# Attention steps in rounds of two, split first maxima, and roots as plain products, in a hybrid diffusion block

## The chip, the cores and the metric

The kernel runs on one core of one Trainium2 chip. The time is device microseconds of one execution of the whole program; lower is better. Before the change it is 1875.17 us, the median of three runs (1874.18 to 1875.43).

The engines have short names in the profile: PE is TensorE (PEld its weight loads), DVE VectorE, ACT ScalarE, POOL GpSimd, SP the engine that issues transfers. PE multiplies a stationary operand (weights, up to 128 rows and 128 columns) with a moving one and writes into banks of its result memory, of 512 fp32 columns each. A product with fewer rows or columns uses a part of the array, and the profile names the form: `128*128` is the whole array, `64*128` one half of the rows, `128*64` one half of the columns.

## What is computed

Two layers over 512 latent and 256 context tokens of width 1024: grouped-query attention with normed and rotated queries and keys, then a bidirectional Mamba-2 mixer, each followed by a gated feed-forward layer. The change touches attention, and the row norms of all layers.

```python
def rms_norm(x, g):
    xf = x.astype(jnp.float32)
    y = xf * lax.rsqrt(jnp.mean(xf * xf, axis=-1, keepdims=True) + EPS)
    return (y * g.astype(jnp.float32)).astype(x.dtype)

def gqa_attend(q, k, v):
    s = jnp.einsum('bqhgd,bkhd->bhgqk', q, k).astype(jnp.float32) * (HEAD_DIM ** -0.5)
    p = jax.nn.softmax(s, axis=-1).astype(v.dtype)
    return jnp.einsum('bhgqk,bkhd->bqhgd', p, v)

    q_l = rms_norm(q_l.reshape(bsz, seq, N_HEADS, HEAD_DIM), q_norm)
...
    k_all = jnp.concatenate([k_l, k_c], axis=1)
    v_all = jnp.concatenate([v_l, v_c], axis=1)
...
    ob = lax.map(lambda qblk: gqa_attend(qblk, k_all, v_all), qb)
```

There are 16 query heads of 64 channels and 4 key heads. Latent queries see all 768 keys, context queries the 256 context keys.

## The kernel before

Tokens lie along columns, channels along partitions. fp32 operands of the large products are split into a high and a low part of a faster type (float32r), and each product is three: high by high, low by high, high by low (`mm3`, lines 108, 109, 111). Products that stay in plain fp32 show as two PE records each; transposes and float32r products as one.

**Heads in pairs.** Two query heads lie on the two halves of the partitions, so that their score products use the two halves of the array's rows. A `Pair` has two generators:

- `maxima` finds, for each query, a bound of its scores ahead of the exponentials. It has seven parts; each writes score products (`ps_m`, line 625) into a two-bank buffer, and DVE reduces it to maxima (line 627). At the end the row `diag` is made of them (line 648).
- `steps` has seven steps, one for each block of 128 keys for latent queries, and a last one for context queries. A step makes the scores transposed (`ps_s`, lines 697 and 699: eight products of 512 columns, the last two add the maxima from `diag`), ACT takes the exponential into `pr` (line 700), and DVE adds it to `acc`. The step hands back a function, `later`, that multiplies `pr` with the values (`ps_o`, `ps_oc`, line 661) and, at the end, divides by the sums (`ps_sum`).

**The loop** (line 809) goes over eight pairs. For each step t of pair p it emits the step's scores, then one part of the next pair's maxima, then the `later` of the step before, so that the exponential has a step's time. Then comes other work: the preparation of queries of later pairs (`prep`), and fill: projections of queries (`ps_q`), modulation products (`ps_ada`), and in pairs 6 and 7 the output projection (`ps_d`).

**Buffers.** The result memory has two two-bank buffers (`S`), taken in turn by `ps_s` and `ps_m`, and four single banks (`Bank`), for `ps_o`, `ps_q`, `ps_ada`, sums and roots.

**Roots.** `rstd_rows` (line 235) gives the reciprocal roots of mean squares. Per token they come out as columns; they are needed as rows, equal over 128 partitions (c = 1, the norms of whole tokens: tiles rsa, `rsTa`, `rsTf`, `rsTs`, `rsTy`) or over each half of 64 (c = 2, head norms: `rsTq`, ten times six). A transpose of a column that is repeated 128 times does it (line 266). For c = 2 DVE first writes the repeated columns out into a wide tile, `rbq` (line 259).

**What sets the order.** Within an engine, instructions run in the order of the program. Where the kernel gives no order by hand, a scheduler sets it from the order of emission and from its own estimates; `behind(a, b)` keeps a behind b.

Of the kernel before, what the change touches and what calls it, by code (L numbers as in the profile page):

```python
# [7 lines left out]
P = 128  # L8
# [3 lines left out]
ALU = mybir.AluOpType  # L12
AX = mybir.AxisListType
# [54 lines left out]
def t3(g, name, dt=F32, n=T):  # L68
    return g.t3p.tile([P, n], dt, tag="t3", bufs=g.n3, name=name)
# [165 lines left out]
def rstd_rows(g, sq, n, cols, width, name, bank):  # L235

    nc = g.nc
    c = cols.shape[-1]  # L240
    nt = n // P
    ps = bank(f"ss{name}")
    for t in range(nt):
        nc.tensor.matmul(ps[:, t * c : (t + 1) * c], sq[:, t * P : (t + 1) * P], cols, start=True, stop=True)
    small = lambda nm: g.p.tile([P, nt * c], F32, tag="rst", bufs=8, name=nm)
    a, y, u = small("rsa"), small("rsy"), small("rsu")
    nc.vector.tensor_scalar(a, ps[:, : nt * c], 1.0 / width, EPS, ALU.mult, ALU.add)

    for f in ((lambda: nc.scalar.activation(y, a, AF.Ln)), (lambda: nc.scalar.activation(y, y, AF.Exp, scale=-0.5))):
        follow(g, f()) if g.tables else f()  # L250
    nc.vector.tensor_tensor(u, y, a, ALU.mult)
    nc.vector.scalar_tensor_tensor(u, y, -0.5, u, ALU.mult, ALU.mult)
    if c == 1:
        nc.vector.scalar_tensor_tensor(a, u, 1.5, y, ALU.add, ALU.mult)
        root = lambda t: a[:, t : t + 1].broadcast_to([P, P])
    else:
        rb = t3(g, f"rb{name}", n=n)
        wide = lambda v: v.unsqueeze(2).broadcast_to([P, nt * c, P // c])
        nc.vector.scalar_tensor_tensor(rb.rearrange("p (a b) -> p a b", b=P // c), wide(u), 1.5, wide(y),
                                       ALU.add, ALU.mult)  # L260
        root = lambda t: rb[:, t * P : (t + 1) * P]
    yield BREAK
    for t0 in range(0, nt, 4):
        pt = bank(f"rsT{name}")
        for t in range(t0, min(nt, t0 + 4)):
            nc.tensor.transpose(pt[:, (t - t0) * P : (t - t0 + 1) * P], root(t), g.ident)
        yield (pt, t0 * P, min(n, (t0 + 4) * P))


# [122 lines left out]
def attention(g, fill, X, late):  # L392


    nc, I = g.nc, g.I
# [209 lines left out]
        nc.gpsimd.tensor_copy(id2[h], g.ident[h, h])  # L605
    small = lambda name, dt=F32: g.p.tile([P, 2, T // P], dt, tag="mx", bufs=4, name=name)

    class Pair:


# [4 lines left out]
        def maxima(self):  # L615


            qh, kh = qprep[self.p][0], [h for h, _ in k2[self.kv]]
            lat, ctx, mz = small("ma"), small("mb"), small("mz")

            def scores(ts, k0, n, out):
                ps = Sb("ps_m")
                for i, t in enumerate(ts):
                    for e in range(2):
                        nc.tensor.matmul(ps[:, 512 * e + n * i : 512 * e + n * i + n], qh[S64[e], t * P : (t + 1) * P],
                                         kh[e][S64[e], k0 : k0 + n], start=True, stop=True)
                nc.vector.reduce_max(out[:, :, ts[0] : ts[-1] + 1], ps.rearrange("p (e t k) -> p e t k", e=2, k=n),
                                     axis=AX.X, negate=True)

            scores((4, 5), L, C, lat)  # L630
            nc.vector.tensor_copy(ctx[:, :, 4:], lat[:, :, 4:])
            yield
            for t in (0, 2):
                scores((t,), 0, L, lat)
                yield
                scores((t + 1,), 0, L, lat)
                yield
                scores((t, t + 1), L, C, ctx)
                if t:

                    for e in range(2):
                        for h in range(2):
                            nc.vector.tensor_tensor(mz.rearrange("p h t -> p t h")[S64[e], :, h], lat[S64[h], e],
                                                    ctx[S64[h], e], ALU.min)
                    self.diag = g.t3p.tile([P, T], F32R, tag="mrow", bufs=2, name=f"diag{self.p}")
                    v = self.diag.rearrange("p (t h q) -> p t h q", h=2, q=64)
                    for h in range(2):
                        nc.vector.tensor_tensor(v[:, :, h], id2.unsqueeze(1).broadcast_to([P, T // P, 64]),
                                                mz[:, h].unsqueeze(2).broadcast_to([P, T // P, 64]), ALU.mult)
                yield  # L650

        def steps(self):
# [5 lines left out]
            def values(po, pr, t, off, n, first, last):  # L658
                v = vt[t][:, self.kv * HD : (self.kv + 1) * HD]
                for e in range(2):  # L660
                    nc.tensor.matmul(po[S64[e], :n], v, pr[:, 512 * e + off : 512 * e + off + n], start=first, stop=last)  # L661

            def final(po, ps, acc, out):

# [25 lines left out]
            for t in range(7):  # L690
                ps, pr = Sb("ps_s"), g.t3p.tile([P, 1024], F32, tag="pr", bufs=3, name="pr")
                for q0, n, k0, off in (((0, L, t * P, 0),) if t < 6 else ((L, C, L, 0), (L, C, L + P, C))):
                    q, k = slice(q0, q0 + n), slice(k0, k0 + P)
                    outs = [ps[:, 512 * e + off : 512 * e + off + n] for e in range(2)]
                    for i, (a, b) in enumerate(((0, qh), (1, qh), (0, ql))):
                        for e in range(2):
                            nc.tensor.matmul(outs[e], kk[e][a][S64[e], k], b[S64[e], q], start=i == 0, stop=False)  # L697
                    for e in range(2):
                        nc.tensor.matmul(outs[e], onesr[S64[e]], self.diag[S64[e], q], start=False, stop=True)  # L699
                exps.append(nc.scalar.activation(pr, ps, AF.Exp))  # L700
# [12 lines left out]
                yield (lambda t=t, pr=pr, po=po, acc=acc: later_lat(po, pr, t, acc)) if t < 6 else (  # L713
                    lambda pr=pr, acc=acc: later_ctx(pr, acc))
# [25 lines left out]
    def ofetch(p):  # L740
        od[p] = t3(g, f"od{p}")
        nc.sync.dma_start(od[p], odram[p])
# [66 lines left out]
    for p in range(NH // 2):  # L809
        m = iter(())  # L810
        if p < 7:
            m = pairs[p + 1].maxima()
        for t, todo in enumerate(pairs[p].steps()):
            next(m, None)
            if late_step:
                late_step()
            late_step = todo
            if p < 6:
                if t in (0, 3, 4, 5):
                    next(prep[p])  # L820
                if t == 6:
                    for _ in prep[p]:
                        pass
                    if p == 5:
                        ofetch(0)
                spread(1.04 if p < 5 else 0.62)
                continue
            if p == 6 and t < 5:
                if t < 4:
                    ofetch(t + 1)  # L830
                osplit(t)
                wos.append(load_w(g, I["w_o"][t * P : (t + 1) * P], after=exps[-1]))
            if p == 6 and t == 2:
                late(wos[:3], (0, 1, 2))
            if p == 6 and t == 4:
                late(wos[3:], (3, 4))
            if p == 7 and t == 2:
                ofetch(5)
            if p == 7 and t == 3:
                osplit(5)  # L840
                osplit(6)
            if p == 6 and t < 3:
                spread(0.62)
                if t == 2:
                    for _ in side:
                        pass
                    for _, gen in tails:
                        for _ in gen:
                            pass
            else:  # L850
                fill.run(3.5)
    late_step()
    osplit(7)

# [675 lines left out]
```

## Time and profile before

| | |
|---|---|
| median of three runs | 1875.17 us |
| the profiled execution | 1875.38 us |
| its span, first to last instruction | 1873.6 us |
| granted TensorE clock | 0.998 |
| attention with heads (the loop over pairs) | about 111 to 367 us of the span |

A row of the timeline has start and duration in us, engine, line, operation, output and inputs, the form of the array, the shape, and how many equal ones are merged in it. Matmuls are pipelined, so durations overlap: what a product holds PE for is the difference of two starts. A row of a group has, behind the bar, busy us and mean ns of one, then the idle time in front of it and what ended it.

### The profile page before, as it was taken

How to read it: one execution, taken by the hardware profiler on the slowest of the kernel's cores; microseconds unless marked ns; L12 is line 12 of the kernel's file. 1: busy time of each engine (PE TensorE's matmuls, PEld its weight loads, DVE VectorE, ACT ScalarE, POOL GpSimd, SP SyncE). 2: the span in 40 equal slices, each digit the busy share in tenths (PEclk: the TensorE clock that was granted, in tenths of full speed). 3: DMA queues.
4: the chain of work that ended last, by engine and by line, in shares of the span. 5: the costliest groups of instructions: out<-in, count | busy, mean ns of one | idle time of the engine just before them, and what ended most of it. 6: DMA issues, size and time to landing. Idle time of an engine off the chain costs nothing.

```text
span 1873.6 us, 28798 instructions
## 1 busy us (share of the span) xinstructions
PE 1848.9 (99%) x11474; PEld 1547.2 (83%) x11474; DVE 1303.6 (70%) x1950; ACT 807.3 (43%) x1402; POOL 299.8 (16%) x266
## 2 busy tenths in 40 slices
PE   9999999999999999999999999999999999999999
PEld 8876656798888888888888888888887888888887
DVE  6588888778787776544487787777797565565655
ACT  4534444363122222222367667776666352323231
POOL 2123120040000000000032333444443210000000
PEclk9999999999999999999999999999999999999999
DMA  9233151124444552211224432443352223222232
GB/s 345 76 109 101 63 178 52 57 84 164 146 135 145 191 185 99 68 58 56 68 91 141 124 105 87 124 124 113 124 178 93 79 91 97 95 95 97 90 103 89
DMA packets 74070, 211.67 MB, mean 113 GB/s; under 512 B 9040, under 2 KB 14544, under 8 KB 73808
## 3 DMA queue, kind: packets, MB, share of 16 engines
q1 hardware_dynamic: 73936, 209.84, 34.0%
q8 instruction: 90, 1.47, 0.3%
q14 instruction: 44, 0.36, 0.1%
HBM read 198.79 MB, written 6.82 MB: 110 GB/s over the span
## 4 chain that ended last, share of the span: by engine, by line
PE 84%; DVE 7%; issue 3%; DMA 2%; POOL 2%; ACT 2%; SPq 0%; DVEq 0%; POOLq 0%; ACTq 0%
PE ps_up L108 10%; PE ps_up L111 10%; PE ps_up L109 10%; PE ps_d L108 6%; PE ps_d L111 6%; PE ps_d L109 6%; PE ps_in L111 4%; PE ps_in L109 4%; PE ps_in L108 4%; PE ps_s L697 2%; PE ps_o L661 2%; PE ps_st L1123 2%; DMA wada<-in_adaA 1%; PE ps_wo L111 1%; PE ps_wo L108 1%
## 5 line engine op out<-in xcount | busy, mean ns | idle before, releaser
L87 DVE TENSOR_TENSOR wl<-wst,wh 128x1024 fp32r<-128x1024 f32 x207 | 258.5, 1249 | 233.9 <-PE ps_up L109 138.9
L85 ACT CAST wh<-wst 128x1024 fp32r<-128x1024 f32 x211 | 221.3, 1049 | 393.7 <-DMA wst<-in_wup 323.6
L108 PE MATMUL ps_up<-hhf,wh 128*128 128x512 f32 x1008 | 357.6, 355 | 0.0
L109 PE MATMUL ps_up<-hlf,wh 128*128 128x512 f32 x1008 | 357.3, 354 | 0.0
L111 PE MATMUL ps_up<-hhf,wl 128*128 128x512 f32 x1008 | 357.0, 354 | 0.0
L108 PEld LDWEIGHTS ps_up<-hhf,wh 128*128 128x128 f32 x1008 | 190.8, 189 | 26.4
L109 PEld LDWEIGHTS ps_up<-hlf,wh 128*128 128x128 f32 x1008 | 190.8, 189 | 26.3
L111 PEld LDWEIGHTS ps_up<-hhf,wl 128*128 128x128 f32 x1008 | 190.6, 189 | 26.4
L108 PE MATMUL ps_in<-hhs,wh 128*128 128x512 f32 (+1 forms) x560 | 204.4, 365 | 1.5 <-ACT dt L1008 1.5
L109 PE MATMUL ps_in<-hls,wh 128*128 128x512 f32 (+1 forms) x560 | 199.4, 356 | 0.0
L111 PE MATMUL ps_in<-hhs,wl 128*128 128x512 f32 (+1 forms) x560 | 198.7, 355 | 0.0
L108 PE MATMUL ps_d<-hdh,wh 128*128 128x512 f32 (+1 forms) x568 | 193.3, 342 | 0.2 <-ACT hdh L85 0.2
L111 PE MATMUL ps_d<-hdh,wl 128*128 128x512 f32 (+1 forms) x568 | 193.5, 341 | 0.0
L109 PE MATMUL ps_d<-hdl,wh 128*128 128x512 f32 (+1 forms) x568 | 192.9, 340 | 0.3 <-DVE hdl L87 0.3
L874 DVE SCALAR_TENSOR_TENSOR X<-ps_d,mod,X 128x512 f32<-128x512 f32 (+1 forms) x224 | 124.3, 583 | 35.9 <-PE ps_d L111 35.2
L108 PEld LDWEIGHTS ps_in<-hhs,wh 128*128 128x128 f32 x560 | 105.9, 189 | 16.6 <-ACT dt L1008 1.7
L109 PEld LDWEIGHTS ps_d<-hdl,wh 128*128 128x128 f32 x568 | 106.7, 188 | 14.8 <-DVE hdl L87 0.7
L111 PEld LDWEIGHTS ps_in<-hhs,wl 128*128 128x128 f32 x560 | 105.8, 189 | 14.7
L111 PEld LDWEIGHTS ps_d<-hdh,wl 128*128 128x128 f32 x568 | 106.6, 188 | 13.1
L108 PEld LDWEIGHTS ps_d<-hdh,wh 128*128 128x128 f32 x568 | 106.3, 188 | 13.4 <-ACT hdh L85 0.7
L109 PEld LDWEIGHTS ps_in<-hls,wh 128*128 128x128 f32 x560 | 106.0, 189 | 13.2
L700 ACT ACTIVATE pr<-ps_s 128x1024 f32<-128x1024 f32 x56 | 57.2, 1021 | 107.2 <-PE ps_s L699 107.2
(339 smaller groups left out, 3653.4 us busy)
## 6 DMA issues: line engine op xcount, KB each, us to landing
wst<-in_wup SPq DMA_DIRECT2D x88, 512.0 KB, 3.3
wada<-in_adaT SPq DMA_DIRECT2D x56, 512.0 KB, 3.3
wst<-in_win SPq DMA_DIRECT2D x48, 512.0 KB, 3.4
wst<-in_wdown SPq DMA_DIRECT2D x44, 512.0 KB, 3.5
E<-ad SPq DMA_DIRECT2D x64, 256.0 KB, 6.9
wada<-in_adaB SPq DMA_DIRECT2D x24, 512.0 KB, 4.1
ec<-ead SPq DMA_DIRECT2D x64, 128.0 KB, 5.6
wst<-in_wout SPq DMA_DIRECT2D x16, 512.0 KB, 3.3
```

What stands on the lines that cost most here:

```text
L85: cast = keep(nc.scalar.copy(hi, src))
L87: keep(eng.tensor_tensor(lo, src, _r(hi), ALU.subtract))
L108: mm(out, wh, ah, start=first, stop=False)
L109: mm(out, wh, al, start=False, stop=False)
L111: mm(out, wl, ah, start=False, stop=last)
L661: nc.tensor.matmul(po[S64[e], :n], v, pr[:, 512 * e + off : 512 * e + off + n], start=first, stop=last)
L697: nc.tensor.matmul(outs[e], kk[e][a][S64[e], k], b[S64[e], q], start=i == 0, stop=False)
L700: exps.append(nc.scalar.activation(pr, ps, AF.Exp))
L874: nc.vector.scalar_tensor_tensor(ap, o[:, c0:c1], gate[:, m, v : v + 1], ap, ALU.mult, ALU.add)
L1123: nc.tensor.matmul(ps[:, d * 256 : (d + 1) * 256], Bt[:, t * P : (t + 1) * P], xw[d][t], start=t == ts[0], stop=t == ts[-1])
```

## The change

Three things are changed.

1. The loop over a pair's seven steps goes in rounds: steps (0, 1), (2, 3), (4, 5), (6). In a round of two, both steps' scores come first, then two parts of the next pair's maxima, then the `later` of the step before the round and that of the first step, and then the other work of both. In the last round, the maximum comes ahead of the step.
2. The first part of the maxima in such a round no longer uses a two-bank buffer. It takes two single banks; a product of 2 by 2 on the lower 64 rows is written into the second bank in front of it, and DVE reduces each bank by itself. The values are kept behind the last scores (`rows64`).
3. `rstd_rows` has no wide tile and no transposes: each root column, read with a stride of zero, is the stationary operand of a plain fp32 product with the identity, over 128 columns for c = 1, and as two products with 64 columns each for c = 2.

```diff
-    if c == 1:
-        nc.vector.scalar_tensor_tensor(a, u, 1.5, y, ALU.add, ALU.mult)
-        root = lambda t: a[:, t : t + 1].broadcast_to([P, P])
-    else:
-        rb = t3(g, f"rb{name}", n=n)
-        wide = lambda v: v.unsqueeze(2).broadcast_to([P, nt * c, P // c])
-        nc.vector.scalar_tensor_tensor(rb.rearrange("p (a b) -> p a b", b=P // c), wide(u), 1.5, wide(y),
-                                       ALU.add, ALU.mult)
-        root = lambda t: rb[:, t * P : (t + 1) * P]
+    nc.vector.scalar_tensor_tensor(a, u, 1.5, y, ALU.add, ALU.mult)
+    w = P // c
...
-            nc.tensor.transpose(pt[:, (t - t0) * P : (t - t0 + 1) * P], root(t), g.ident)
+            for j in range(c):
+                nc.tensor.matmul(pt[j * w : j * w + w, (t - t0) * P : (t - t0 + 1) * P],
+                                 a[:, t * c + j : t * c + j + 1].broadcast_to([P, w]), g.ident, start=True, stop=True)
...
+    rows64, single = [None], [False]
...
-                ps = Sb("ps_m")
+                if single[0]:
+                    pe = [Bk("ps_m") for _ in range(2)]
+                    nc.tensor.matmul(pe[1][:2, :2], onesr[S64[1], :2], onesr[S64[1], :2], start=True, stop=True)
+                else:
+                    ps = Sb("ps_m")
+                    pe = [ps[:, :512], ps[:, 512:]]
...
+                if single[0]:
+                    for e in range(2):
+                        nc.vector.reduce_max(out[:, e, tt], pe[e][:, : n * len(ts)].rearrange("p (t k) -> p t k", k=n),
+                                             axis=AX.X, negate=True)
...
-                    nc.tensor.matmul(po[S64[e], :n], v, pr[:, 512 * e + off : 512 * e + off + n], start=first, stop=last)
+                    behind(g, nc.tensor.matmul(po[S64[e], :n], v, pr[:, 512 * e + off : 512 * e + off + n], start=first, stop=last),
+                           rows64[0])
...
-        for t, todo in enumerate(pairs[p].steps()):
-            next(m, None)
+        steps = pairs[p].steps()
+        for ts in ((0, 1), (2, 3), (4, 5), (6,)):
+            if len(ts) == 1:
+                next(m, None)
+            todo = [next(steps) for _ in ts]
+            if len(ts) == 2:
+                for single[0] in (True, False):
+                    next(m, None)
             if late_step:
                 late_step()
-            late_step = todo
...
+            for step in todo[:-1]:
+                step()
+            late_step = todo[-1]
+            for t in ts:
```

What the change does to the order on PE is seen in the middle of pair 1. Before, from the scores of one step to those of the next (ps_s scores, ps_m maxima, ps_o values, ps_ada fill, rsTq roots):

```order
L697 MATMUL ps_s<-ql,khs_1139 128x512
L699 MATMUL ps_s<-diag_1754,onesr 128x512 x2
L625 MATMUL ps_m<-khs_1139,qh 128x512
L625 MATMUL ps_m<-kh_1137,qh 128x512
L661 MATMUL ps_o<-pr,v_909 64x512 x2
L132 MATMUL ps_ada<-wada,sc_83 32x128 x32
L697 MATMUL ps_s<-qh,kh_1137 128x512
```

Each step goes from scores and maxima (half the rows) to values (half the columns) to other work and back. The same place now, from the first step's last scores:

```order
L708 MATMUL ps_s<-diag_1767,onesr 128x512 x2
L706 MATMUL ps_s<-qh,kh_1147 128x512
L706 MATMUL ps_s<-qh,khs_1149 128x512
L706 MATMUL ps_s<-qh,kl_1148 128x512
L706 MATMUL ps_s<-qh,kls_1150 128x512
L706 MATMUL ps_s<-ql,kh_1147 128x512
L706 MATMUL ps_s<-ql,khs_1149 128x512
L708 MATMUL ps_s<-diag_1767,onesr 128x512 x2
L621 MATMUL ps_m<-onesr 2x2
L627 MATMUL ps_m<-khs_1149,qh 128x512
L627 MATMUL ps_m<-kh_1147,qh 128x512
L627 MATMUL ps_m<-khs_1149,qh 128x256
```

The second step's scores follow the first's at once, then the 2 by 2 product, the first part of the maxima (512 columns) and the second (256). What follows them there:

```order
L627 MATMUL ps_m<-kh_1147,qh 128x256
L669 MATMUL ps_o<-pr,v_909 64x512 x2
L669 MATMUL ps_o<-pr,v_910 64x512 x2
L132 MATMUL ps_ada<-wada,sc_83 32x128 x32
L260 MATMUL rsTq<-cst,rsa 64x128 x8
L706 MATMUL ps_s<-qh,kh_1147 128x512
```

Two steps' values stand together, and the roots are eight products of 64 rows where four transposes of 128 rows stood (`rsTq<-cst,rbq 128x128 x4`).

On DVE, the second and third step of pair 2 before, with sums (acc), maxima (ma, mb) and the multiplication with the roots (qs):

```order
L627 TENSOR_REDUCE ma<-ps_m 128x2
L707 TENSOR_TENSOR acc<-acc,pr 128x1024
L627 TENSOR_REDUCE mb<-ps_m 128x2x2
L707 TENSOR_TENSOR acc<-acc,pr 128x1024
L552 TENSOR_TENSOR qs<-qs,rsTq 128x512
```

And now:

```order
L716 TENSOR_TENSOR acc<-acc,pr 128x1024
L632 TENSOR_REDUCE ma<-ps_m 128x1 x2
L716 TENSOR_TENSOR acc<-acc,pr 128x1024
L635 TENSOR_REDUCE mb<-ps_m 128x2x2
L547 TENSOR_TENSOR qs<-qs,rsTq 128x512
```

The first part of the maxima is two reductions of one bank each, and the second is behind the second step's sum.

More of the change, by code (lines that the diff above doesn't have):

```diff
@@ L698, in steps @@
                     for e in range(2):
-                        nc.tensor.matmul(outs[e], onesr[S64[e]], self.diag[S64[e], q], start=False, stop=True)
+                        rows64[0] = nc.tensor.matmul(outs[e], onesr[S64[e]], self.diag[S64[e], q], start=False, stop=True)
                 exps.append(nc.scalar.activation(pr, ps, AF.Exp))
@@ L812, in attention @@
             m = pairs[p + 1].maxima()
-        for t, todo in enumerate(pairs[p].steps()):
-            next(m, None)
+        steps = pairs[p].steps()
[6 more added lines that the diff above has]
+                    next(m, None)
             if late_step:
                 late_step()
-            late_step = todo
[L818 to L848, printed above, removed]
-                            pass
-            else:
-                fill.run(3.5)
@@ new lines, in attention @@
+            for step in todo[:-1]:
+                step()
+            late_step = todo[-1]
+            for t in ts:
+                if p < 6:
+                    if t in (0, 3, 4, 5):
+                        next(prep[p])
+                    if t == 6:
+                        for _ in prep[p]:
+                            pass
+                        if p == 5:
+                            ofetch(0)
+                    spread(1.04 if p < 5 else 0.62)
+                    continue
+                if p == 6 and t < 5:
+                    if t < 4:
+                        ofetch(t + 1)
+                    osplit(t)
+                    wos.append(load_w(g, I["w_o"][t * P : (t + 1) * P], after=exps[-1]))
+                if p == 6 and t == 2:
+                    late(wos[:3], (0, 1, 2))
+                if p == 6 and t == 4:
+                    late(wos[3:], (3, 4))
+                if p == 7 and t == 2:
+                    ofetch(5)
+                if p == 7 and t == 3:
+                    osplit(5)
+                    osplit(6)
+                if p == 6 and t < 3:
+                    spread(0.62)
+                    if t == 2:
+                        for _ in side:
+                            pass
+                        for _, gen in tails:
+                            for _ in gen:
+                                pass
+                else:
+                    fill.run(3.5)
@@ L852, in attention @@
+        next(steps, None)
     late_step()
```

10 lines of the change are left out of this document (6 added, 4 removed).

## The prediction

> **What bounds the kernel now.** I read the page's busy times first, then its chain of waits.
>
> ```profile
> PE 1848.9 (99%) x11474; PEld 1547.2 (83%) x11474; DVE 1303.6 (70%) x1950; ACT 807.3 (43%) x1402; POOL 299.8 (16%) x266
> ...
> PE 84%; DVE 7%; issue 3%; DMA 2%; POOL 2%; ACT 2%; SPq 0%; DVEq 0%; POOLq 0%; ACTq 0%
> ```
>
> TensorE (PE) is busy for 99% of the span and holds 84% of the chain. So a microsecond of PE is a microsecond of the kernel, and the other engines count only where PE waits for them. Where it waits in the attention stage, which the change rewrites, is seen by stretches (columns: PE, PEld, DVE, ACT, POOL busy, then clock and DMA):
>
> ```profile
> 112.00:230.00 118.00, 117.34 (x873) 72.26 (x872) 97.17 (x135) 53.27 (x73) 26.62 (x16) 1.00 0.28 93
> 230.00:262.00 32.00, 31.29 (x291) 19.58 (x294) 24.69 (x43) 13.32 (x22) 4.96 (x3) 1.00 0.33 116
> 262.00:296.00 34.00, 30.86 (x319) 16.56 (x311) 31.42 (x49) 15.98 (x22) 5.69 (x3) 1.00 0.49 170
> ```
>
> PE is idle for 0.66, 0.71 and 3.14 us in these; the last stretch (the end of pair 5, the start of pair 6) is where VectorE (DVE) is full, 31.42 of 34 us. Everywhere else PE is the limit, at a granted clock of 1.00. But "busy" hides something. The timeline of one step (start, duration) shows it in the starts:
>
> ```profile
> 181.24 0.39 PE L111 MATMUL ps_q<-hha,wl 128*128 128x512 f32 x1
> 181.56 0.50 PE L697 MATMUL ps_s<-qh,khs 64*128 64x512 f32 x1
> ...
> 181.90 0.40 PE L697 MATMUL ps_s<-qh,kls 64*128 64x512 f32 x1
> ...
> 182.13 0.39 PE L697 MATMUL ps_s<-ql,kh 64*128 64x512 f32 x1
> ...
> 182.59 0.27 PE L625 MATMUL ps_m<-kh,qh 64*128 64x256 f32 x1
> ...
> 182.93 1.08 PE L661 MATMUL ps_o<-pr,v 128*64 128x512 f32 x4
> 183.94 0.66 PE L266 MATMUL rsTq<-cst,rbq 128*128 128x128 f32 x4
> ```
>
> Two score products, one on each half of the array's rows (`64*128`), run as a pair, and pairs follow each other by 0.23 us (181.90 to 182.13). Where the form of the array changes, `128*128` to `64*128`, the last old product holds 0.32 us instead of 0.23, and the first new pair holds 0.34 (181.56 to 181.90). So a change of form costs about 0.09 on the way out, plus 0.11 before a form with 128 columns gets going: **0.20 us into `64*128`**. The way into `128*64` is read from the one place where two value groups stand together:
>
> ```profile
> 280.08 1.08 PE L661 MATMUL ps_o<-pr,v 128*64 128x512 f32 x4
> 280.99 1.03 PE L667 MATMUL ps_sum<-acc,ones 128*64 128x512 f32 x4
> 281.95 0.43 PE L132 MATMUL ps_ada<-wada,sc 128*32 128x128 f32 x8
> ```
>
> Eight records take 1.87 us here; four alone take 1.01 (182.93 to 183.94). Twice 1.01 less 1.87 is **0.15 us into `128*64`**.
>
> **The change part by part.** *Rounds.* Two steps' scores, two maxima and two steps' values now follow each other, so forms change less often. Counted over both programs: into `64*128` 65 times before, 44 after (those behind the new small product apart); into `128*64` 73 and 62; into `128*128` 80 and 73; into `128*32` 14 and 14. I take 0.20 for `128*128` as well (the two rows behind ps_y below: 0.33 against 0.23, and 0.09 on the way out). Gain: 21 x 0.20 + 11 x 0.15 + 7 x 0.20 = **-7.25 us**. It all lies on PE, nothing hides it.
>
> *The small product.* 21 rounds have one, 2x2 on 64 rows, in form `64*32`, between scores and maxima that both have form `64*128`. No row of before has this change of form. Two changes cost 0.09 in, and 0.09 + 0.11 out; its own time I take from the nearest narrow products:
>
> ```profile
> 250.22 1.96 PE L132 MATMUL ps_ada<-wada,sc 128*32 128x128 f32 x64
> 252.11 0.38 PE L697 MATMUL ps_s<-qh,kh 64*128 64x256 f32 x1
> ```
>
> 1.89 us for 64 records, 0.03 each. So 0.32 x 21 = **+6.7 us**. The low end is 0.03 x 21 = 0.6, if a form that keeps its 64 rows changes without the array running empty; `128*128` to `128*64` keeps its rows too and does pay (ps_yo to ps_y in the rows below: eight records of ps_yo hold 0.98 us, 1042.54 to 1043.52, and 0.89 in front of an equal form, 0.81 and 0.08 on the next product), so I take the high end. The Trainium skill ("TensorEngine Tiling (Array Packing)", Key Properties) says that changing the tiling mode, not just the tile, drains the array, and its list has 64x128 and 64x32 as two modes; the trace has no such pair, and by the page the sum stays as it is.
>
> *Roots.* Before, six transposes per generator; now twelve plain fp32 products, each with two records:
>
> ```profile
> 78.39 0.82 PE L266 MATMUL rsTq<-cst,rbq 128*128 128x128 f32 x6
> 78.96 0.37 PE L108 MATMUL ps_c<-hha,wsh 128*128 128x256 f32 x1
> 79.17 0.28 PE L109 MATMUL ps_c<-hla,wsh 128*128 128x256 f32 x1
> ...
> 1033.31 1.05 PE L1188 MATMUL ps_yo<-Cf,hs 128*128 128x128 f32 x8
> 1034.12 0.36 PE L108 MATMUL ps_in<-hhs,wh 128*128 128x256 f32 x1
> 1034.32 0.28 PE L109 MATMUL ps_in<-hls,wh 128*128 128x256 f32 x1
> ...
> 1042.54 1.05 PE L1188 MATMUL ps_yo<-Cf,hs 128*128 128x128 f32 x8
> 1043.52 1.09 PE L1197 MATMUL ps_y<-E,xt 128*64 128x128 f32 x16
> 1044.55 0.50 PE L108 MATMUL ps_in<-hhs,wh 128*128 128x512 f32 x1
> 1044.88 0.39 PE L109 MATMUL ps_in<-hls,wh 128*128 128x512 f32 x1
> 1045.11 0.40 PE L111 MATMUL ps_in<-hhs,wl 128*128 128x512 f32 x1
> ```
>
> Six transposes hold PE 0.57 us, and the product behind them 0.09 more than its usual 0.12: 0.66, or 0.11 each. The new form has an exact twin, ps_y: `128*64`, 128 columns, fp32, alternating column halves. Its 16 records are eight products in 1.03 us, less 0.15 for the change of form: 0.11 per product. Twelve make 1.32. The difference is 0.66 for each of ten generators: **+6.6 us**. Where one root serves all 128 columns the transpose becomes a plain `128*128` product, twin ps_yo: four products in 0.81 + 0.08, so 0.22 against 0.11. The groups:
>
> ```profile
> L266 PE MATMUL rsTq<-cst,rbq 128*128 128x128 f32 x60 | 10.3, 286 | 0.0
> L266 PE MATMUL rsTf<-cst,rsa 128*128 128x128 f32 x10 | 2.1, 292 | 1.0 <-DVE rsa L254 0.9
> L266 PE MATMUL rsTs<-cst,rsa 128*128 128x128 f32 x6 | 1.2, 288 | 0.1
> L266 PE MATMUL rsTa<-cst,rsa 128*128 128x128 f32 x6 | 1.0, 272 | 0.0
> L266 PE MATMUL rsTy<-cst,rsa 128*128 128x128 f32 x4 | 0.6, 272 | 0.0
> ```
>
> Ten, six, six and four, 26 x 0.11 = **+2.9 us**.
>
> *Other engines.* DVE loses the wide multiply of the roots and splits 21 maxima in two:
>
> ```profile
> L259 DVE SCALAR_TENSOR_TENSOR rbq<-rsu,rsy x10: 957/958/1634, 73.3 to 262.2; 128x768 f32<-128x768 f32 x10
> ...
> L627 DVE TENSOR_REDUCE ma<-ps_m 128x2 f32<-128x1024 f32 x32 | 39.1, 1221 | 9.3 <-PE ps_m L625 9.2
> ...
> L1190 DVE TENSOR_TENSOR ec<-ec,ps_yo 128x512 f32<-128x512 f32 x32 | 21.1, 678 | 5.3 <-PE ps_yo L1188 5.3
> ```
>
> About 10 x 0.8 less and 21 x 0.14 more (a half maximum estimated at 0.68, from the row of 512 columns read from the same memory). PE covers both, except in the stretch from 262 us; nothing is counted, bounds -1 and +1.
>
> *A new wait.* The second maximum of a round takes the buffer that the first step's exponential must free. That exponential:
>
> ```profile
> 182.81 1.02 ACT L700 ACTIVATE pr<-ps_s 128x1024 f32<-128x1024 f32 x1 [2.96 <-PE ps_s L699]
> ```
>
> It starts 1.25 us behind its scores (181.56) and ends at 2.27. PE gets to the second maximum at 1.03 + 0.92 (two steps' scores), 0.21 (small product) and 0.34 (first maximum): 2.50. So 0.23 us to spare, counted at nothing. Queued behind this maximum are both steps' values, and the next round behind those. Next round's second scores wait for the second maximum's reduction; DVE needs, with 1.22 for any 1024 columns, 2.44 for two sums and 2 x 0.68 + 1.22 for maxima, 5.0 us a round, against PE's 1.95 + 0.21 + 0.57 + 1.87 = 4.6 and the fill. With fill that is covered; without it (pair 5) PE waits as it does now.
>
> Sum: -7.25 + 6.7 + 6.6 + 2.9 = **+8.95 us**. The profiled execution took 1875.38 (span 1873.6 and 1.8 around it), 0.2 above the median of 1875.17; from the median: **1884.1 us**.
>
> **The rivals.** *The small product is cheap.* No drain within 64 rows: 0.6 instead of 6.7. Then PE comes to the second maximum at 1.95 + 0.03 + 0.23 = 2.21, in front of the exponential's end at 2.27, and waits about 0.1 with the release, 21 x 0.1 = 2.1. Together 4.0 less: 1880.1. For it: both forms use the same 64 rows. Against it: ps_yo to ps_y.
>
> *The rounds take PE's waits away.* This one ends not slower. PE waits today for exponentials and reductions:
>
> ```profile
> PEld ps_s L697 <- ACT pr L700: 5.6, 5, 2.3
> ...
> PEld ps_m L625 <- DVE ma L627: 2.5, 2, 2.2
> ```
>
> Two steps' work in a row could cover all 8.1 us of it: 1876.0, within the noise of before. It decides once it brings over 5.2 us (then the loss is below 0.2%). For it: DVE loses 5 us in all. Against it: the waits lie where DVE is full, and PE's idle time there is only 3.14 us.
>
> *Exponentials come late.* 0.23 us is little, since ScalarE has casts in the same queue:
>
> ```profile
> L85 ACT CAST wh<-wst 128x1024 fp32r<-128x1024 f32 x211 | 221.3, 1049 | 393.7 <-DMA wst<-in_wup 323.6
> ```
>
> One in front of an exponential now stops PE at once, where before a whole step lay between. If a third of 21 rounds meet a full one, 7 x (1.05 - 0.23) = 5.7: 1889.8. Pair 6, where each step brings casts of weights and outputs, is the likeliest place. For it: the queue is in order, and nothing lets an exponential pass. Against it: ScalarE is busy for less than half of the time (53.27 of 118 us, and 15.98 of 34 in the rows above).
>
> **How the numbers follow.** The forecast has a chance of 0.52, the cheap small product 0.18, the waits gone 0.17, late exponentials 0.13. The range goes from below the third case's full effect, 1875, to a little above the last, 1891. Slower or faster by 0.2% (3.75 us, about what can be told from no change) is 1878.9 and 1871.4. Slower has all of the first and last case and 0.11 of the second: 0.76. No change has 0.10 of the third and 0.07 of the second: 0.17. Faster is what is left of the third, where the small product would be cheap as well: 0.07.
>
> **What would show it.** Right: ps_m products of 2x2 with about 0.3 us between the last scores and the first maximum; two value groups in 1.87; ps_s pairs of two steps without a gap; 12 root products in about 1.3 us; rsTf at 0.22 each. Wrong: a gap under 0.1 us around the small product (then 4 us less), PE's idle share between 262 and 296 us gone, or new waits of PE for pr.

## The result, and the profile after

The changed kernel takes **1887.22 us** (median of four runs, 1885.38 to 1887.59); the kernel before took 1875.3 on the same chip (four runs, 1874.18 to 1876.1). The ratio is **1.0064, 95% interval [1.0048, 1.0080]**: slower by 12 us. The forecast was 1884.1 with a range of 1875.0 to 1891.0. The total is near, but three of its terms are off (the saved changes of form, the small product and a new wait), and their errors partly cancel: that the sum comes so near is luck.

The page of the profiled execution (span 1885.8 us, clock 0.999), busy times and shares of the chain of waits:

```profile
PE 1858.0 (99%) x11701; PEld 1562.7 (83%) x11701; DVE 1298.4 (69%) x1971; ACT 807.0 (43%) x1402; POOL 298.4 (16%) x266
...
PE 82%; DVE 9%; issue 3%; ACT 3%; POOL 1%; DMA 1%; SPq 0%; DVEq 0%; POOLq 0%; ACTq 0%
```

PE grew by 9.1 us, DVE fell by 5.2, and DVE's share of the chain rose from 7% to 9%: DVE does less and is waited for more. The stretches of attention (columns: PE, PEld, DVE, ACT, POOL busy, clock, DMA):

```profile
112.00:230.00 118.00, 114.36 (x919) 77.11 (x919) 90.26 (x137) 47.84 (x67) 31.32 (x16) 1.00 0.27 85
230.00:262.00 32.00, 31.97 (x234) 20.68 (x236) 23.13 (x38) 11.98 (x18) 3.79 (x3) 0.95 0.16 54
262.00:296.00 34.00, 32.05 (x430) 20.80 (x423) 28.00 (x54) 15.37 (x21) 3.80 (x3) 1.00 0.61 218
```

In the first stretch PE now stands idle for 3.64 us, where it was 0.66. DVE is busy there for 90 of 118 us, so it isn't full: it is late. The second stretch had a granted clock of 0.95 in this execution, against 1.00 before, which makes its products longer (figures further down). PE's waits from 112 to 384 us by what ended them (us in total, times, longest):

```profile
PE ps_s L706 <- DVE ma L635: 2.0, 2, 1.3
PE ps_d L108 <- DVE ma L632: 1.3, 1, 1.3
PE ps_s L706 <- DVE mb L635: 1.3, 1, 1.3
PE ps_m L627 <- DVE qs L547: 1.2, 1, 1.2
...
PE ps_m L627 <- ACT pr L709: 0.3, 1, 0.3
```

Scores (`ps_s`, line 706) wait 3.3 us for the reduction of a second maximum (line 635), whose buffer they take. Here is one of these places, the round from 152.2 us and the next; PE first (start, duration; in brackets an idle time and what ended it):

```profile
153.90 0.41 PE L708 MATMUL ps_s<-diag,onesr 64*128 64x512 f32 x2
154.14 0.39 PE L627 MATMUL ps_m<-khs,qh 64*128 64x512 f32 x1
154.16 0.16 PE L621 MATMUL ps_m<-onesr 64*2 64x2 f32 x1
154.18 0.47 PE L627 MATMUL ps_m<-kh,qh 64*128 64x512 f32 x1
154.51 0.38 PE L627 MATMUL ps_m<-khs,qh 64*128 64x256 f32 x1
...
154.94 1.94 PE L669 MATMUL ps_o<-pr,v 128*64 128x512 f32 x8
156.81 1.95 PE L132 MATMUL ps_ada<-wada,sc 128*32 128x128 f32 x64
158.70 1.09 PE L260 MATMUL rsTq<-cst,rsa 128*64 128x128 f32 x16
159.72 0.50 PE L706 MATMUL ps_s<-qh,kh 64*128 64x512 f32 x1
...
160.52 0.39 PE L708 MATMUL ps_s<-diag,onesr 64*128 64x512 f32 x2
162.19 0.50 PE L706 MATMUL ps_s<-qh,kh 64*128 64x512 f32 x1 [1.28 <-DVE mb L635]
```

Several steps of the prediction are seen at once: two value groups in 1.87 us (154.94 to 156.81), eight root products in 1.02 (158.70 to 159.72). The 2 by 2 product has a gap of 0.02 us on either side, not 0.3. And the second scores of the next round come at 162.19 instead of 160.75. What DVE did in that time, and GpSimd beside it:

```profile
154.49 1.98 DVE L716 TENSOR_TENSOR acc<-acc,pr 128x1024 f32<-128x1024 f32 x1 [2.92 <-ACT pr L709]
156.39 1.27 DVE L632 TENSOR_REDUCE ma<-ps_m 128x1 f32<-128x512 f32 x2
157.59 3.41 DVE L716 TENSOR_TENSOR acc<-acc,pr 128x1024 f32<-128x1024 f32 x1
160.93 1.21 DVE L635 TENSOR_REDUCE mb<-ps_m 128x4 f32<-128x1024 f32 x1
```

```profile
154.11 1.28 POOL L541 TENSOR_TENSOR raw<-raw,cs 128x512 f32<-128x512 f32 x1 [33.10 <-DMA qsw<-raw]
155.35 2.25 POOL L542 TENSOR_TENSOR qsw<-qsw,cs 128x512 f32<-128x512 f32 x1
157.57 2.35 POOL L87 TENSOR_TENSOR wl<-wst,wh 128x1024 fp32r<-128x1024 f32 x1
159.89 2.24 POOL L543 TENSOR_TENSOR raw<-raw,qsw 128x512 f32<-128x512 f32 x1
```

The two sums (`acc`) take 1.98 and 3.41 us, and the reduction of the second maximum, which PE is waiting for, stands behind both in DVE's queue. The reductions take their usual time. The theory after this reading: the roots cost about what was forecast, the small product much less, and the missing part is a wait that has two conditions, the order of the sum on DVE and GpSimd's work beside it.

### The profile page after: what moved, and what is told of

It is laid out like the page before. It is cut to its first block, busy times and chain, and to the rows that moved or that the text cites. A ratio compares the mean times of both kernels' runs of the same rounds, so it can differ in the third digit from the quotient of the medians.

```text
span 1885.8 us, 29272 instructions
## 1 busy us (share of the span) xinstructions
PE 1858.0 (99%) x11701; PEld 1562.7 (83%) x11701; DVE 1298.4 (69%) x1971; ACT 807.0 (43%) x1402; POOL 298.4 (16%) x266
## 4 chain that ended last, share of the span: by engine, by line
PE 82%; DVE 9%; issue 3%; ACT 3%; POOL 1%; DMA 1%; SPq 0%; DVEq 0%; POOLq 0%; ACTq 0%
PE ps_up L111 10%; PE ps_up L109 10%; PE ps_up L108 10%; PE ps_d L108 6%; PE ps_d L111 6%; PE ps_d L109 6%; PE ps_in L111 4%; PE ps_in L109 4%; PE ps_in L108 4%; PE ps_s L706 2%; PE ps_o L669 2%; PE ps_st L1142 2%; PE ps_wo L111 1%; PE ps_wo L108 1%; PE ps_wo L109 1%
## 5 line engine op out<-in xcount | busy, mean ns | idle before, releaser
L170 DVE SCALAR_TENSOR_TENSOR junk<-wada,cb 128x1024 f32<-128x1024 f32 x80 | 97.4, 1217 | 1.1 <-ACT cb L162 0.8
```

Source lines behind the costliest of these rows:

```text
L170: g.tc.keep_in_program_order(nc.vector.scalar_tensor_tensor(junk, w, 1.0, cb[:, v * D : (v + 1) * D], ALU.mult, ALU.mult, accum_out=md[:, ...
```

## The experiments

Twelve kernels ran, in sets on several chips. The kernel before ran beside each set and its median was between 1873.8 and 1875.8 us, so between sets the ratio to it is the better measure. The granted clock isn't the same everywhere either: it was 0.995 to 0.998 in the runs of e1, 0.998 to 1.000 in those of the change, e2, e3 and e4.

| run | median us | ratio to before, 95% interval |
|---|---|---|
| the change | 1887.22 | 1.0064 [1.0048, 1.0080] |
| e1_old_roots | 1880.51 | 1.0027 [1.0016, 1.0038] |
| e2_new_roots | 1884.35 | 1.0048 [1.0035, 1.0060] |
| e3_no_small | 1887.59 | 1.0067 [1.0055, 1.0080] |
| e4_sum_last | 1883.61 | 1.0044 [1.0030, 1.0057] |
| e5_rounds_sum_last | 1872.48 | 0.9982 [0.9974, 0.9991] |
| e6_small64 | 1887.58 | 1.0063 [1.0047, 1.0078] |
| e6b_small128 | 1890.47 | 1.0077 [1.0063, 1.0091] |
| e8_pool_idle | 1882.32 | 1.0031 [1.0019, 1.0043] |
| e9_rounds_but_pair6 | 1869.48 | 0.9975 [0.9966, 0.9984] |
| e10_two_bank | 1879.37 | 1.0028 [1.0018, 1.0039] |
| e11_token_roots | 1877.95 | 1.0020 [1.0011, 1.0029] |
| e12_with_small | 1874.20 | 0.9996 [0.9987, 1.0005] |

**The roots.** In `e1_old_roots` the changed kernel has the `rstd_rows` of before:

```diff
-            for j in range(c):
-                nc.tensor.matmul(pt[j * w : j * w + w, (t - t0) * P : (t - t0 + 1) * P],
-                                 a[:, t * c + j : t * c + j + 1].broadcast_to([P, w]), g.ident, start=True, stop=True)
+            nc.tensor.transpose(pt[:, (t - t0) * P : (t - t0 + 1) * P], root(t), g.ident)
```

> The changed kernel with the roots of before (transposes of a wide tile); rounds and small products stay. By the prediction's sum the new roots cost 6.6 + 2.9 = 9.5 us, so this run should be near 1877.7. By the trace of after (ten generators at 0.66 us, and +0.9 us in the part of the program behind attention where the roots of whole tokens stand) they cost about 8, so 1879. Rival: the loop waits for DVE, and the products of the eight generators inside it lie in those waits; then only the two generators ahead of the loop and the whole-token roots count, about 3 us, and this run gives 1884.

`e2_new_roots` is the reverse: the kernel before with the new `rstd_rows`, and nothing else.

> The kernel before with the new roots alone. Prediction's sum: +9.5 us, 1884.8. Trace of after: +8 us, 1883.3. Rival, roots covered by waits in the loop, or paid back by DVE's lost wide multiply (ten times about 1 us): +3 us or less, 1878.

`e11_token_roots` gives the kernel before plain products for the roots with c = 1 only:

```diff
+            if c == 1:
+                nc.tensor.matmul(pt[:, (t - t0) * P : (t - t0 + 1) * P], root(t), g.ident, start=True, stop=True)
+            else:
+                nc.tensor.transpose(pt[:, (t - t0) * P : (t - t0 + 1) * P], root(t), g.ident)
```

> The kernel before with plain products for the roots of whole tokens alone (26 products in place of transposes); the head roots stay transposes of the wide tile. Prediction's term: 26 x 0.11 = +2.9 us, 1878.6. By the times of the rest of the program in the traces (1506.8 before, 1507.7 to 1508.2 with the new roots): +1.4, 1877.1. Rival: nothing, they lie where PE waits for the row norms anyway: 1875.7.

Alone the new roots cost 8.7 us (1884.35 less 1875.62 of before beside it; 6.6 to 11.3 by the interval), 9.5 were forecast. The roots of whole tokens cost 3.8 by their ratio (2.1 to 5.4), 2.9 were forecast; the +1.4 that I read from one pair of traces lies outside. Within the rounds the roots make a difference of 6.7 us (1887.22 less 1880.51), or 8.4 where the two ran at the same granted clock (below). The rivals of +3 us or less fall.

**The small product.** `e3_no_small` takes the line out:

```diff
-                    nc.tensor.matmul(pe[1][:2, :2], onesr[S64[1], :2], onesr[S64[1], :2], start=True, stop=True)
```

> The changed kernel without the 2 by 2 product in front of the first maxima. By the prediction each costs 0.32 us, so 21 x 0.32 = 6.7 us less: 1880.5. By the trace of after the product itself holds 0.02 us and the pair behind it 0.13 us more than usual: 21 x 0.13 = 2.7 us less, 1884.5. Rival: the second maximum then waits so much longer for the first step's exponential, and nothing is gained: 1886.5 to 1888.

Nothing is gained, as the rival had it. PE's weight loads, which overlap with its products, wait for the exponential ahead of the maxima, in the changed kernel first, then without the small product:

```profile
PEld ps_m L627 <- ACT pr L709: 2.4, 12, 0.5
```

```profile
PEld ps_m L626 <- ACT pr L708: 5.9, 18, 0.6
```

12 waits of 2.4 us in all become 18 of 5.9: the maxima come a little earlier, and their weight loads wait longer. So the product's own price has to be measured where no wait stands behind it. `e6_small64` adds 24 such products in front of the second scores of a round; `e6b_small128` has the same with `onesr[:, :2]`, over 128 rows:

```diff
+                if t in (1, 3, 5):
+                    nc.tensor.matmul(ps[:2, 512:514], onesr[S64[1], :2], onesr[S64[1], :2], start=True, stop=True)
```

> The changed kernel with 24 more 2 by 2 products on the lower 64 rows, one in front of the second scores of each round, where PE waits for nothing behind it; they write a corner of the bank that the scores overwrite. Prediction's price of the form 64*32 between two 64*128 forms: 24 x 0.32 = 7.7 us, 1895. Price seen in the trace of after (0.02 us in, 0.13 out): 24 x 0.15 = 3.6, 1891. Rival: nothing at all, since PE's later waits take it up: 1887 to 1888.

> The same 24 products at the same place, over all 128 rows instead of 64: the only difference to the run before is that the rows of the array change as well. If a change of rows empties the array and a change of columns alone doesn't, this is slower than the run on 64 rows by 24 x (0.09 + 0.09) = 4.3 us or more; if both do, the two are equal; by the prediction's price 1895.

On 64 rows, 24 products cost 0.4 us together, which is nothing that can be measured; on 128 rows 3.3, or 2.9 more than the run on 64 rows beside it. The timeline on 64 rows:

```profile
152.54 0.40 PE L710 MATMUL ps_s<-diag,onesr 64*128 64x512 f32 x2
152.77 0.39 PE L708 MATMUL ps_s<-qh,kh 64*128 64x512 f32 x1
152.78 0.16 PE L702 MATMUL ps_s<-onesr 64*2 64x2 f32 x1
152.80 0.47 PE L708 MATMUL ps_s<-qh,khs 64*128 64x512 f32 x1
153.01 0.39 PE L708 MATMUL ps_s<-qh,kl 64*128 64x512 f32 x1
153.12 0.39 PE L708 MATMUL ps_s<-qh,kls 64*128 64x512 f32 x1
```

And on 128 rows:

```profile
153.83 0.41 PE L710 MATMUL ps_s<-diag,onesr 64*128 64x512 f32 x2
154.17 0.17 PE L702 MATMUL ps_s<-onesr 128*2 128x2 f32 x1
154.27 0.49 PE L708 MATMUL ps_s<-qh,kh 64*128 64x512 f32 x1
154.27 0.49 PE L708 MATMUL ps_s<-qh,khs 64*128 64x512 f32 x1
154.60 0.39 PE L708 MATMUL ps_s<-qh,kl 64*128 64x512 f32 x1
```

On 64 rows the upper half goes on at its own pace (152.77, 153.01); the lower half is 0.11 us behind it (153.12) and stays so: the two halves are staggered, and the array as a whole isn't emptied. On 128 rows the last scores hold 0.34 instead of 0.23, the product 0.10, the next pair 0.33 instead of 0.23: 0.31 us, about the price of the prediction. Of 24 x 0.31 = 7.4 us only about 3 reach the time; that later waits take up the rest is likely, but no run shows it. The Trainium skill ("TensorEngine Tiling (Array Packing)", Key Properties) says that a change of tiling mode drains the array; the runs agree where the product takes 128 rows instead of 64, and not where it stays on its 64 rows and only the columns change.

**The late reduction.** `e4_sum_last` emits the sum of a round's second step behind the maxima:

```diff
-                    nc.vector.tensor_tensor(acc, acc, pr, ALU.add)
+                    self.add = lambda acc=acc, pr=pr: nc.vector.tensor_tensor(acc, acc, pr, ALU.add)
+                    if t != 3 and t != 5:
+                        self.add()
...
                 for single[0] in (True, False):
                     next(m, None)
+                pairs[p].add()
```

(and the same deferral for t = 1).

> The changed kernel with one order changed: the sum of a round's second step is emitted behind the round's maxima, so that on DVE the reduction of the second maximum stands ahead of it. If the new waits of PE (second scores of a round for a buffer that this reduction frees) come from the reduction standing behind a sum that waits for the second exponential, about 5 us go: 1882. Rival: DVE is simply fuller in the rounds, and slowed beside GpSimd, so that the waits move to the sums or to the next reduction: 1886 to 1888. A third way: the later sum delays the next round, slower than 1889.

3.6 us less, and the runs of the two kernels don't overlap (1881.99 to 1884.17 against 1885.38 to 1887.59). The intervals of the ratios do, but e3, which ran beside e4, lies above it as well (1885.84 to 1889.79). The same stretch and the waits of PE in this run:

```profile
112.00:230.00 118.00, 117.49 (x953) 79.58 (x953) 89.34 (x143) 51.25 (x72) 28.53 (x16) 1.00 0.30 94
```

```profile
PE ps_m L627 <- DVE qs L547: 1.8, 1, 1.8
PE ps_d L108 <- DVE ma L632: 1.2, 1, 1.2
PE ps_m L627 <- ACT pr L709: 0.5, 1, 0.5
PE ps_d L111 <- DVE wl L87: 0.4, 1, 0.4
```

PE's idle time in the stretch falls from 3.64 to 0.51 us, and the scores' waits for a maximum are gone from the list. `e8_pool_idle` tests the other condition. GpSimd's rotation in the loop is left out, and the low part of the query weights is set to zero:

```diff
-        eng.tensor_tensor(qs[:, :L], qs[:, :L], g.cos, ALU.mult)
-        eng.tensor_tensor(sw, sw, g.sin, ALU.mult)
-        eng.tensor_tensor(qs[:, :L], qs[:, :L], sw, ALU.add)
+        if eng is nc.vector:
+            eng.tensor_tensor(qs[:, :L], qs[:, :L], g.cos, ALU.mult)
+            eng.tensor_tensor(sw, sw, g.sin, ALU.mult)
+            eng.tensor_tensor(qs[:, :L], qs[:, :L], sw, ALU.add)
```

> The changed kernel with GpSimd's work of the loop left out: the three tensor products of the rotation of queries and keys prepared there aren't done, and the low part of the query weights is set to zero instead of a difference. If DVE's sums of 1.22 us that took up to 3.4 us in the trace of after were slowed by GpSimd beside them, their mean goes from 1.50 to about 1.25 us, the waits of PE for the reductions behind them go, and the time falls by 2.5 to 4 us: 1883 to 1885. Rival: the sums are long for another reason, or PE's waits come from the wait for the second exponential alone: 1886.5 to 1888.

4.9 us less (6.2 by the ratios), more than expected. The group of the sums (busy us, mean ns of one), in the kernel before, in the changed kernel, and in this run:

```profile
L707 DVE TENSOR_TENSOR acc<-acc,pr 128x1024 f32<-128x1024 f32 x32 | 41.8, 1307 | 4.3 <-ACT pr L700 4.3
```

```profile
L716 DVE TENSOR_TENSOR acc<-acc,pr 128x1024 f32<-128x1024 f32 x32 | 47.9, 1497 | 29.7 <-ACT pr L709 29.6
```

```profile
L720 DVE TENSOR_TENSOR acc<-acc,pr 128x1024 f32<-128x1024 f32 x32 | 39.0, 1220 | 32.3 <-ACT pr L713 32.2
```

GpSimd is busy in the loop for 2.9 us here (it still writes the zeros), where it was 37.5, and every sum takes its 1.22 us. So both conditions hold: the sums are long because GpSimd works beside them, and this reaches PE because the reduction is queued behind them. Taking away either one gives back 3.6 or 4.9 us. Other DVE work has no part in it: DVE's busy time in the loop falls by 8.8 us (203.7 to 194.9), and the sums' by 8.9. But one other wait has: the 1.2 us in which PE waited for the queries that GpSimd rotates (`ps_m` for `qs` in the list of the changed kernel) are gone as well, so that some 3.7 of the 4.9 us are left for the late reduction.

**The rounds by themselves.** `e5_rounds_sum_last` has three of the edits above together: old roots, no small product, the sum behind the maxima.

> The changed kernel with the roots of before, without the 2 by 2 product, and with the second step's sum behind the maxima: the rounds with single banks and nothing else. If the three edits add, from the runs so far (rounds with old roots 1880.5, sum order -3.6, small product 0): 1876.9, no better than before. If the saved changes of form (the prediction's 7.25 us) are there and only the waits of the sum's order hid them: 1870 to 1872. If the single banks make waits of their own (fill and roots that wait for a bank which a reduction holds): 1878 or more.

1872.48: faster than before, by 3.4 us of 1875 (1.7 to 4.9). The edits don't just add to 1876.9. To see which of them gives more together than alone, `e12_with_small` puts the 2 by 2 product back into this kernel.

> The run of rounds with old roots and the sum behind the maxima, but with the 2 by 2 product kept, which e5 left out: does the product cost something once the late reductions no longer hide it? If it is free as in e3, 1872.5 and a ratio of 0.998. If the difference between e4 and e5 (11.1 us, 2.4 more than the roots cost alone) is the product's, 1875, ratio 1.000. By the prediction's price of 6.7 us: 1879, ratio 1.002.

1874.20: 1.7 us more than e5 by the medians, 2.6 by the ratios, whose intervals touch; far from 6.7. The traces don't show even this as the product's price: pairs 0 to 4 take the same time as in e5 (31.81, 28.83, 28.80, 27.62 and 28.85 us, against e5's row in the table below). The difference lies in pairs 5 and 6, where PE waits 2.3 us for `qs` instead of 1.0, and the granted clock was 0.92 (284 to 327 us) instead of 0.96.

The runs now form a path: 1875.3 before, 1872.5 with rounds, single banks and the sum behind the maxima (e5), 1874.2 with the small product (e12), 1880.5 with the sum in its old place (e1), 1887.2 with the new roots (the change). The steps are -2.8, +1.7, +6.3 and +6.7 (by the ratios -3.4, +2.6, +5.8 and +6.9). By way of e4 instead of e1, the last two are +9.4 for the roots and +3.6 for the sum's place. That looks as if either cost less with the other there, but e1 ran at the lowest clock of all. The runs at a clock of 0.998 alone (medians of 1874.2 for e12, 1879.1 for e1 and 1883.6 for e4, and one run of the change, 1887.5) give +5.0 and +8.4 on the first way, +9.4 and +3.9 on the second. So the late reduction is worth about 4 to 5 us and the new roots 8 to 9, and it isn't shown that the one changes the price of the other. `e10_two_bank` is e5 with both maxima of a round set back into two-bank buffers:

```diff
-                for single[0] in (True, False):
+                for single[0] in (False, False):
```

> The run of rounds with old roots, no small product and the sum behind the maxima (1872.5), but both maxima of a round take two-bank buffers, as before the change. Both buffers are then full of a round's scores, the first maximum waits for the first exponential (0.3 us behind) and the second for the second exponential (about 0.7 us more): 21 x 1.0 = 21 us more at most, 1893; with fill pulled ahead of the maxima by the scheduler about half, 1882. Rival: no difference, the single banks bring nothing: 1872 to 1874.

6.9 us slower than e5 by the medians, 8.6 by the ratios: near the half of the 21 us that was expected with fill ahead of the maxima. PE's waits, its weight loads ahead of the products:

```profile
PEld ps_m L631 <- ACT pr L713: 17.3, 28, 1.3
PE ps_m L631 <- ACT pr L713: 6.1, 24, 0.9
```

PE waits 24 times for an exponential, 6.1 us: with both two-bank buffers full of scores the maxima can't start before an exponential is done. Without the single banks the rounds lose more than they bring.

Pair by pair, from the trace (us between the starts of the pairs' last sum products, `ps_oc<-accc`, the first from the first scores; the fill in each pair is the same in all). In rounds a pair's end lies behind one more step of scores (0.92 us), which counts for pair 0 and against pair 7:

| pair | 0 | 1 | 2 | 3 | 4 | 5 | 6 | 7 |
|---|---|---|---|---|---|---|---|---|
| before | 30.97 | 28.65 | 29.72 | 28.49 | 29.69 | 27.38 | 38.60 | 42.08 |
| the change | 31.89 | 31.55 | 31.52 | 28.67 | 31.26 | 29.20 | 39.19 | 39.52 |
| e2, new roots alone | 30.81 | 29.03 | 30.38 | 29.22 | 30.41 | 28.05 | 38.61 | 42.08 |
| e5 | 31.82 | 28.80 | 28.80 | 27.60 | 28.89 | 27.93 | 41.21 | 39.50 |

e2 shows a generator's 0.66 us in pairs 2 to 5 (0.66, 0.73, 0.72, 0.67). The change's pair 4 ran at the clock of 0.95; e3 has 29.71 us there at 1.00. Four of the ten generators of roots stand ahead of the first scores, which come at 115.3 us instead of 111.2, so the pairs hold only 7.2 of the 12 us.

In e5 pairs 2 to 4 gain 0.8 to 0.9 each, and pair 6 seems to lose 2.6. But the granted clock fell there, as it did at the same place in e12 and not in the change or in e3 (columns as above, the whole pair and 4 us of it):

```profile
284.30:325.50 41.20, 39.08 (x192) 22.82 (x190) 33.22 (x50) 17.10 (x26) 0.00 (x0) 0.96 0.21 71
294.00:298.00 4.00, 4.00 (x12) 2.03 (x11) 3.76 (x5) 0.18 (x1) 0.00 (x0) 0.57 0.67 263
```

Products of 512 columns follow each other there by 0.42 us (295.11 to 295.53) instead of 0.23. At 0.57, 4 us lose about 1.7 (an estimate), so some 0.9 us are left for the order of work; whether the rounds bring on the fall of the clock isn't known. `e9_rounds_but_pair6`, built on the reading of 2.6, is e5 with pair 6 in single steps (inside it the order of a step is that of before):

```diff
-        for ts in ((0, 1), (2, 3), (4, 5), (6,)):
+        for ts in ((0, 1), (2, 3), (4, 5), (6,)) if p != 6 else [(t,) for t in range(7)]:
```

> The run of rounds with old roots, no small product and the sum behind the maxima (1872.5), but pair 6, counted from 0, goes in single steps as before the change. In the traces pair 6 is the one pair that the rounds make longer (38.6 us before, 41.2 with them), so if that comes from its rounds, 2.6 us less: 1870. Rival: the pair's casts of weights cost the same whichever order, or the loss moves into the next pair: 1872 to 1873.

1869.48, 0.9975 of before [0.9966, 0.9984]: the fastest of all, and clearly ahead of both kernels. Against e5 it isn't settled: the ratios' intervals overlap, and the two ran beside different sets. In its trace, at a clock of 1.00, pairs 5 and 6 take 66.31 us together, against 69.14 in e5, of which 1.7 are the clock, and 65.98 before.

## Why the prediction was right, and where it wasn't

- **Roots, +6.6 and +2.9:** right in mechanism, a little high in place. 8.7 alone (6.6 to 11.3), of it 3.8 (2.1 to 5.4) for the tokens' roots; 6.7 to 9.4 within the rounds. The twins `ps_y` and `ps_yo` gave the price: eight products in 1.02 us, against 8 x 0.11 and 0.15 for the form.
- **Small product, +6.7:** mis-sized; 0 in the change (e3), 0.4 for 24 of them (e6), and nothing in pairs 0 to 4 where the waits are mended (e12), whose whole time is 1.7 to 2.6 longer for reasons that aren't shown to be the product. The step that failed is "`128*128` to `128*64` keeps its rows too and does pay", and with it "so I take the high end". Keeping all 128 rows is not the same as keeping one half: with two halves at work, one goes on while the other changes. The rival of the cheap product named this, and also that PE then waits for the exponential.
- **New wait, 0:** wrong; 3.6 us by e4, 5.0 to 6.3 by e12 and e1. The step that failed is "With fill that is covered". The rule before it was right, that the next round's second scores wait for the second maximum's reduction; the price of the sums, "2.44 for two", was not. At 154.49 us, where the round began at 152.20, DVE took 1.98 and 3.41 for the two, 2.95 more. It was done at 162.14, and PE was there at 160.75; with the usual sums DVE would have been done at 159.19, in time. The group of before, with a mean of 1307 ns against the 1220 of a sum alone, had hinted at it; I took the short one.
- **Forms, -7.25:** the sign is shown, the term is mis-sized. e5 gives -2.8 to -3.4, with what waits are left in it, and more was due there: the prediction's count takes in the changes of form that the new roots add. Counted in e5's trace, with the old roots, PE goes 44 times into `64*128`, 51 into `128*64` and 67 into `128*128`, by the prediction's prices 21 x 0.20 + 22 x 0.15 + 13 x 0.20 = 10.1; the new roots put 2.85 back. Pair 7, which has no maxima, gains 2.58, less the 0.92 of the boundary, 1.66. Seven steps in four rounds spare three of each change of form, by the prices 3 x (0.20 + 0.15 + 0.20) = 1.65. But pairs 2 and 3, where PE stands idle for 0.1 us at most, spare three of each as well and gain only 0.92 and 0.89, and pairs 0, 1, 5 and 6 gain next to nothing or lose. So the step that failed is the sum's, one price for every change of form, with "It all lies on PE, nothing hides it"; which of the two gives way, and where, is open.
- **The rivals.** "Waits gone" went the other way. Idle time of PE from the first scores to the last sums, before and now:

```profile
111.20:366.90 255.70, 251.19 (x1895) 157.74 (x1896) 205.95 (x302) 107.26 (x149) 38.08 (x22) 1.00 0.27 92
```

```profile
115.30:378.20 262.90, 255.29 (x2024) 170.30 (x2025) 203.79 (x322) 106.83 (x149) 37.51 (x22) 0.99 0.27 89
```

4.51 us became 7.61. About 1.5 us of the longer stretch are the lower clock in pair 4 (31.26 us against e3's 29.71). Late exponentials behind casts did little: the only wait for `pr` listed for PE is 0.3 us. The measured time is nearer to that rival's 1889.8 than to the forecast, but by another wait.

- **Sum:** the terms -7.25, +6.7, 0 and +9.5 measured -2.8, +1.7, +6.3 and +6.7 along the path by e1, and -2.8, +1.7, +3.6 and +9.4 by e4. The forecast of +8.95 stands against +11.9 since the small product was priced too high, and the gain of the forms too high and the wait too low. The price of the roots was a good forecast; that the whole comes within about 3 us is luck.

## What to carry to other kernels

When a buffer goes from one user to the next through a reduction, look at what stands in front of that reduction in its engine's queue, and price those at their longest, not their usual, time. Here moving one line in the order of emission was worth about 4 to 5 us. A product that is priced by "a change of form empties the array" needs its own row: here a 2 by 2 product cost 0.31 us on 128 rows between products on 64, and nothing that could be measured where it stayed on one half of the rows. And before a stretch of one trace is compared with the same stretch of another, look at the clock granted in both: in pair 6 of e5 it made some 1.7 of 2.6 us.

## What the runs showed of the hardware

- DVE's sum of two SBUF operands of 128x1024 takes 1.22 us alone, and up to 3.41 with GpSimd's tensor products beside it; GpSimd's own go from 1.28 to 2.25. They take turns: GpSimd's product of 154.11 to 155.39 is followed by the sum's end at 156.47, 1.08 later, and that by GpSimd's next at 157.60. Reductions of DVE that read the result memory stay at 1.21 to 1.22. The Trainium skill ("SBUF — State Buffer", section "SBUF: two separate sides") describes an exclusive lock on a shared port for a DVE operation with two SBUF inputs and one of GpSimd; the trace and e8 (1220 ns for each sum) agree.
- A 2 by 2 product on 64 rows between products on 64 by 128 delays its half by 0.11 us and leaves the other one alone; on 128 rows it costs 0.31.
- The granted clock fell to 0.57 over 294 to 298 us of e5's profiled execution, where products of 512 columns followed each other by 0.42 us instead of 0.23; e3 and e9 show no such fall in the whole loop.
